# Seven-product blocks in a form with four sums on each side: weight sums chained in one tile by adding DMAs, outputs read from running sums in a bank

## The chip, the cores and the metric

One core of one Trainium2 chip. The metric is device time in microseconds (us), the median of several runs of the whole program; smaller is better. All inputs and outputs are float32.

## The reference, cut to what matters

One decoder layer on 512 tokens with 1024 features: retention and dilated attention side by side, a gated merge, then three steps of which the change touches two:

```python
x = x + (gate_r * ret_branch + gate_a * att_branch) @ w_o      # w_o: 1024 x 1024
u = rmsnorm(x, g_mlp) @ w_up                                   # w_up: 1024 x 4096
x = x + jnp.square(jax.nn.relu(u)) @ w_down                    # w_down: 4096 x 1024
gate_p = jax.nn.sigmoid(rmsnorm(x, g_ple) @ w_ple_gate)
return x + gate_p * (p_i @ w_ple_proj)
```

## The kernel before, in words

**Matrix products.** Each float32 operand is split into a high part rounded to fp32r and a low remainder (`hi`, `lo`). `mm3` (L246) makes a product from three matmuls: high by high (L249), high by low (L250), low by high (L251). A weight tile of 128 x 1024 values, 512 KB, is a unit. `fetch` (L187) loads a unit from HBM on the SP queue into one of six `raw` buffers and can add a second block of the weights to it by an adding DMA on the POOL queue (L202). `split_unit` (L223) then writes the high part on ACT (`whi`, L237) and the low one on DVE (`wlo`, L238), into one of four pairs of buffers. A `raw` buffer comes free when its unit is split, a `whi`/`wlo` pair when the matmuls of its unit are done. `units(n)` (L217) hands out the next n units and splits AHEAD units further (2; 3 at the start of the two blocks with a hand-written order).

**Seven-product blocks.** `w_o` (one block) and `w_down` (four blocks of 1024 rows, f = 0 to 3) are done by blocks of 1024 x 1024 in a scheme in the manner of Strassen: the block is cut into 2 x 2 quadrants, and seven products of sums of quadrants replace eight. One block takes 14 units, here called n0 to n13, two for each product m (u = 0 and u = 1). A unit serves 12 matmuls: two output tiles of 128 tokens (p), two row groups (k) and the three of `mm3`. The left-hand sums are made by `seven_left` (L988) on DVE for each of four column groups j = 0 to 3 (`z`, L991 to L995), then split on ACT (`uh`, L998) and DVE (`ul`, L999). Row groups kk = 0, 1 belong to u = 0, and kk = 2, 3 to u = 1, so the last column group j = 3 is needed by every product's second unit.

In `seven_gemm` (L1001) the order is: products 4, 3 and 5 with u = 0, the same three with u = 1, then 2, 1, 7, 6. Products 2, 7 and 6 go on in the banks of 4, 5 and 3. Product 4 is copied out to SBUF (`m4`, L1040) and product 1 is added to it there (L1054). `acc` (L1026) adds a bank or `m4` to the residual `x` on DVE, with the factor of the token. The weight sums are made by eight adding DMAs per block and by two subtractions of whole raw tiles on DVE (L215, from `differences`).

Before a `w_down` block, four calls of `cols_gemm` (L289) compute w_up's columns; each result goes through Relu and Square on ACT (L1113 to L1122) into `seven_left`.

**Order of the work.** A planner orders the instructions of each engine and queue before the program runs, by its own estimate of when they are ready. In two stretches (the `w_o` block with the embedding product, and the last `w_down` block with the gate product) the ACT and DVE orders are those of the program text; PE, SP and POOL stay with the planner. In these two blocks a finished half row of `x` is handed to `gain_T` (L358), which puts four transposes on PE (`split_T`, L325) and two splits on ACT and DVE (L338, L339) in a list; `tick`, called once every six matmuls in the blocks, takes one due entry from that list.

Of the kernel before, what the change touches and what calls it, by code (L numbers as in the profile page):

```python
# [13 lines left out]
AF = mybir.ActivationFunctionType  # L14
ALU = mybir.AluOpType
AX = mybir.AxisListType

P = 128
# [54 lines left out]
def R(ap):  # L73
    return ap.bitcast(F32R)


class Block:


    def __init__(self, ctx, tc, a):  # L80
# [19 lines left out]
        self.differences = {}  # L100
# [63 lines left out]
    def plan_seven(self, w, r0):  # L164


        q = lambda i, j, u: w[r0 + 512 * i + 256 * u : r0 + 512 * i + 256 * (u + 1), 512 * j : 512 * (j + 1)]
        n = len(self.plan)
        for u in range(2):
            self.plan.append(((q(1, 0, u), q(0, 0, u)), None))  # L170
            self.plan.append(((q(0, 1, u), q(1, 1, u)), None))
            self.plan.append((q(1, 1, u), None))
        for u in range(2):
            self.plan.append((q(0, 0, u), None))
        self.differences[n + 7] = [(n + 6 + u, n + 2 + 3 * u) for u in range(2)]
        for u in range(2):
            self.plan.append(((None, n + 6 + u, n + 2 + 3 * u), None))
        for u in range(2):
            self.plan.append(((q(1, 0, u), q(1, 1, u)), None))
        for u in range(2):  # L180
            self.plan.append(((q(0, 0, u), q(0, 1, u)), None))
# [5 lines left out]
    def fetch(self, n):  # L187
        while len(self.raws) < min(len(self.plan), n):
# [4 lines left out]
            if src is None:  # L193
                self.raws.append((self.raws[add[0]][0], add[1]))
                continue
# [9 lines left out]
    def ahead(self, n):  # L205
        while len(self.loaded) < min(len(self.plan), self.used + n):
            i = len(self.loaded)
            self.fetch(i + 1)
            raw, g0 = self.raws[i]
            src = self.plan[i][0]  # L210
            if isinstance(src, tuple) and src[0] is None:
                g0 = None
            self.loaded.append(self.split_unit(raw, g0))
            for v, w in self.differences.get(i, ()):
                self.nc.vector.tensor_tensor(self.raws[v][0], self.raws[v][0], self.raws[w][0], op=ALU.subtract)  # L215
# [280 lines left out]
    def embed(self):  # L496
# [3 lines left out]
        for half in range(2):  # L500
# [5 lines left out]
            self.rows_gemm(([hi], [lo]), 2, store, bank=self.bank)  # L506
# [421 lines left out]
    def mix(self, A, O):  # L928
        nc = self.nc
        U, Z = [[None] * 4, [None] * 4], {}  # L930
        for pair in ((0, 2), (1, 3)):
            parts = {}
            for br, act, nk, bo in (("a", O, H, 24), ("r", A, KD, 16)):
                if pair[0] and br == "r":
                    self.load_x()
                for cc in pair:
# [9 lines left out]
                    def branch(n, ps):  # L946
# [7 lines left out]
                        if kk < 4:  # L954
# [3 lines left out]
                            nc.scalar.activation(z[:, 1], m[:, :256], AF.Copy)  # L958
                            Z[j] = z, m[:, 256:]
                        else:  # L960
                            z, a21 = Z.pop(j)
                            v = lambda ap: ap.rearrange("p (h t) -> p h t", h=2)
                            nc.vector.tensor_tensor(z[:, 0:8:7], v(t), v(parts[kk]), op=ALU.add)
# [24 lines left out]
    def seven_left(self, z, a21, U, j):  # L988

        nc = self.nc  # L990
        sub = lambda o, x, y: nc.vector.tensor_tensor(o, x, y, op=ALU.subtract)  # L991
# [5 lines left out]
        hi, lo, src = w(U[0][j]), w(U[1][j]), z[:, 1:8].rearrange("p a b -> p (a b)")  # L997
        nc.scalar.activation(R(hi), src, AF.Copy)  # L998
        nc.vector.tensor_tensor(R(lo), src, hi, op=ALU.subtract)  # L999

    def seven_gemm(self, U, xs, f, ready):  # L1001


        nc = self.nc
        LEFT = {1: 3, 2: 4, 3: 0, 4: 6, 5: 1, 6: 5, 7: 2}
        banks = {}

        def product(m, bank, u, first, last):
            (wh, wl), = self.units(1)
            for p in range(2):  # L1010
                if first and m != 1:
                    banks[bank, p] = self.gbank() if m in (3, 4) else self.bank("pb")
                ps = banks[bank, p]
                for k in range(2):
                    kk = 2 * u + k
                    c = slice(LEFT[m] * 256 + p * P, LEFT[m] * 256 + (p + 1) * P)
                    sh, sl = (R(U[i][kk].rearrange("p a b -> p (a b)")[:, c]) for i in range(2))
                    self.mm3(ps, sh, sl, wh[:, k], wl[:, k], first and k == 0, last and k == 1, m != bank)
                self.tick()

        X = lambda i, j, p: xs[2 * i + p][:, 512 * j : 512 * (j + 1)]

        def acc(i, j, p, v, sign=0):
            t, x = 2 * i + p, X(i, j, p)
            c = sign * NT + t
            nc.vector.scalar_tensor_tensor(x, v, f[:, c : c + 1], x, op0=ALU.mult, op1=ALU.add)  # L1026

        def done(i, j, p):
            if ready is not None:
                ready(2 * i + p, j, banks.get((1, p)))  # L1030

        for u in range(2):
            for m in (4, 3, 5):
                product(m, m, u, u == 0, u == 1)
        m4 = []
        for p in range(2):
            banks[1, p] = self.bank("pb")
        for p in range(2):
            t = self.tmp("m4")
            nc.scalar.activation(t, banks[4, p], AF.Copy)  # L1040
            m4.append(t)
            acc(0, 1, p, banks[3, p])
            acc(0, 1, p, banks[5, p], 1)
            done(0, 1, p)
        for u in range(2):
            product(2, 4, u, False, u == 1)
        for p in range(2):
            acc(1, 0, p, banks[4, p])
            done(1, 0, p)
            acc(1, 1, p, banks[4, p], 1)  # L1050
        for u in range(2):
            product(1, 1, u, u == 0, u == 1)
        for p in range(2):
            nc.vector.tensor_tensor(m4[p], m4[p], banks[1, p], op=ALU.add)  # L1054
            acc(0, 0, p, m4[p])
            acc(1, 1, p, m4[p])
        self.AHEAD = 2
        for u in range(2):
            product(7, 5, u, False, u == 1)
        for p in range(2):  # L1060
            acc(0, 0, p, banks[5, p])
            done(0, 0, p)
        for u in range(2):
            product(6, 3, u, False, u == 1)
        for p in range(2):
            acc(1, 1, p, banks[3, p])
            done(1, 1, p)


    def tail(self, mx):  # L1070
# [14 lines left out]
        def ready(t, j, free):  # L1085
            late = (t < 2) == (j == 0)
            if not h2:
                h2.extend(self.new_act(2, "h2"))
            self.gain_T(xs[t], t, j, h2, "h2", 2 * j if late else 1 + t // 2,
                        None if late else (lambda s: free) if t < 2 else self.gbank)  # L1090
# [16 lines left out]
        for f in range(NF // 2):  # L1107
# [3 lines left out]
            def act(b, j, ps):  # L1111
                r = self.tmp("ur")
                nc.scalar.activation(r, ps, AF.Relu)  # L1113
                if b == 0:
# [3 lines left out]
                    nc.scalar.activation(z[:, 1], r[:, :256], AF.Square)  # L1118
                    nc.scalar.activation(a21, r[:, 256:], AF.Square)
                else:  # L1120
                    z, a21 = Z[j]
                    nc.scalar.activation(z[:, 0:8:7], r.rearrange("p (h t) -> p h t", h=2), AF.Square)  # L1122
# [6 lines left out]
            if f == NF // 2 - 1:  # L1129
# [3 lines left out]
                def ready(t, j, free):  # L1133
                    late = (t < 2) == (j == 0)
                    self.gain_T(xs[t], t, j, h3, "h3", 0 if late else 1 + t // 2,
                                None if late else (lambda s: free) if t < 2 else self.gbank)
# [34 lines left out]
    def make_plan(self):  # L1171
# [9 lines left out]
        self.plan_seven(a["w_o"][0], 0)  # L1181
        for half in range(2):
            self.plan_rows(a["w_ple_proj"][0], 512 * half, 2)
        for f in range(NF // 2):
# [3 lines left out]
            self.plan_seven(a["w_down"][0], 1024 * f)  # L1188
# [44 lines left out]
```

## Time and profile before

| what | value |
|---|---|
| time, median of 3 runs | 993.74 us (993.59 to 994.11) |
| profiled execution: span from first to last instruction | 991.8 us |
| PE busy | 984.9 us (99%) |
| DVE busy | 648.8 us (65%) |
| ACT busy | 462.1 us (47%) |
| POOL busy | 98.1 us (10%) |
| mean granted TensorE clock | 0.999 |

The page gives no time of its own for the profiled execution beside its span. The median of the runs is 1.94 us above the span, which is what lies outside the first and last instruction. Matmuls overlap in the pipeline, so a PE that is busy all the time can still lose time between starts: the distance from one start to the next says more than the busy share. `whi<-raw` in a row means that the instruction writes `whi` and reads `raw`; x40 is a count.

### The profile page before, as it was taken

To read this page: it belongs to the slowest core of one execution; us is meant where nothing else is said; L and a number is where in the kernel's file an instruction comes from. 1 tells how busy PE (TensorE), PEld (TensorE's weight loads), DVE (VectorE), ACT (ScalarE), POOL (GpSimd) and SP (SyncE) were. 2 spreads that over 40 slices of the span, in tenths; PEclk is the share of its full clock that TensorE was granted. 3 is DMA by queue.
4 is the path that set the end of the run, shared out by engine and by line. 5 is a ranking of instruction groups with operands and counts; after the bars stand their busy time and mean duration, and the time that the engine had idled before them with its cause. 6 is when DMAs were issued, how large, how long until landed. Compare 5 with 4: busy or idle time off the path is not lost.

```text
span 991.8 us, 12456 instructions
## 1 busy us (share of the span) xinstructions
PE 984.9 (99%) x4588; PEld 826.7 (83%) x4588; DVE 648.8 (65%) x1015; ACT 462.1 (47%) x939; POOL 98.1 (10%) x98
## 2 busy tenths in 40 slices
PE   9999999999999999999999999999999999999998
PEld 6888899889888888888888888888888888888886
DVE  7858675774869345454733796678667769767953
ACT  6635344433334334243423448664563565465451
POOL 0310120220000010001002000100101001000000
PEclk9999999999999999999999999999999999999999
DMA  9723122333234322222446486758749767875911
GB/s 333 262 85 87 44 85 85 113 98 98 83 109 153 124 63 76 96 65 86 162 135 156 137 218 201 185 141 221 184 132 226 187 159 170 228 174 128 298 54 54
DMA packets 90910, 141.16 MB, mean 142 GB/s; under 512 B 6320, under 2 KB 40672, under 8 KB 90848
## 3 DMA queue, kind: packets, MB, share of 16 engines
q1 hardware_dynamic: 79824, 119.36, 37.3%
q0 software_dynamic: 10880, 20.97, 12.6%
q8 instruction: 36, 0.59, 0.2%
q14 instruction: 26, 0.21, 0.1%
q10 hardware_dynamic: 144, 0.02, 0.0%
HBM read 136.10 MB, written 4.24 MB: 141 GB/s over the span
## 4 chain that ended last, share of the span: by engine, by line
PE 97%; DVE 1%; ACT 1%; DMA 1%; SPq 0%; issue 0%; ACTq 0%; DVEq 0%
PE pg L249 27%; PE pg L251 27%; PE pg L250 27%; PE pb L251 3%; PE pb L250 3%; PE pb L249 3%; PE po L699 1%; PE ph L555 1%; PE pt L325 1%; PE sc L676 1%; PE ry L905 1%; PE pe L647 1%; PE kv L893 1%; PE sc L682 1%; PE ry L907 1%; DMA raw<-in_w_in 1%
## 5 line engine op out<-in xcount | busy, mean ns | idle before, releaser
L238 DVE TENSOR_TENSOR wlo<-raw,whi 128x1024 fp32r<-128x1024 f32 (+1 forms) x166 | 196.8, 1190 | 104.3 <-ACT whi L237 102.4
L237 ACT ACTIVATE whi<-raw 128x1024 fp32r<-128x1024 f32 (+1 forms) x165 | 169.7, 1033 | 194.9 <-PE pg L251 71.5
L249 PE MATMUL pg<-whi,hh 128*128 128x512 f32 x440 | 177.3, 403 | 0.0
L251 PE MATMUL pg<-whi,hl 128*128 128x512 f32 x440 | 172.2, 391 | 0.0
L250 PE MATMUL pg<-wlo,hh 128*128 128x512 f32 x440 | 171.9, 391 | 0.0
L251 PEld LDWEIGHTS pg<-whi,hl 128*128 128x128 f32 x440 | 90.4, 206 | 15.1
L249 PEld LDWEIGHTS pg<-whi,hh 128*128 128x128 f32 x440 | 90.5, 206 | 13.8
L250 PEld LDWEIGHTS pg<-wlo,hh 128*128 128x128 f32 x440 | 90.7, 206 | 13.6
L249 PE MATMUL pg<-h2h,whi 128*128 128x512 f32 x256 | 99.6, 389 | 0.0
L250 PE MATMUL pg<-h2l,whi 128*128 128x512 f32 x256 | 99.6, 389 | 0.0
L251 PE MATMUL pg<-h2h,wlo 128*128 128x512 f32 x256 | 99.6, 389 | 0.0
L242 ACT ACTIVATE whi<-raw,gcol 128x256 fp32r<-128x256 f32 (+1 forms) x144 | 66.2, 525 | 22.1 <-PE pg L250 12.4
L243 DVE SCALAR_TENSOR_TENSOR wlo<-raw,gcol,whi 128x256 fp32r<-128x256 f32 (+1 forms) x144 | 65.6, 511 | 15.6 <-ACT whi L242 15.6
L202 POOL DMA_DIRECT2D raw<-in_w_down x32 | 38.6, 1206 | 302.8 <-DMA raw<-in_w_down 188.2
L249 PE MATMUL pg<-hh,whi 128*128 128x512 f32 x160 | 64.0, 400 | 0.0
L249 PE MATMUL pg<-whi,uh 128*128 128x512 f32 x160 | 62.8, 393 | 0.1
L251 PE MATMUL pg<-whi,ul 128*128 128x512 f32 x160 | 62.5, 392 | 0.0
L250 PE MATMUL pg<-wlo,uh 128*128 128x512 f32 x160 | 62.5, 391 | 0.0
L251 PE MATMUL pg<-hh,wlo 128*128 128x512 f32 x160 | 62.4, 390 | 0.0
L250 PE MATMUL pg<-hl,whi 128*128 128x512 f32 x160 | 62.3, 389 | 0.0
L250 PEld LDWEIGHTS pg<-h2l,whi 128*128 128x128 f32 x256 | 48.1, 188 | 10.0
L249 PEld LDWEIGHTS pg<-h2h,whi 128*128 128x128 f32 x256 | 48.1, 188 | 9.9
(201 smaller groups left out, 1693.2 us busy)
## 6 DMA issues: line engine op xcount, KB each, us to landing
raw<-in_w_in SPq DMA_DIRECT2D x72, 512.0 KB, 3.9
raw<-in_w_down SPq DMA_DIRECT2D x48, 512.0 KB, 4.3
raw<-in_w_up SPq DMA_DIRECT2D x32, 512.0 KB, 4.8
raw<-in_w_down POOLq DMA_DIRECT2D x32, 512.0 KB, 6.7
raw<-in_w_o SPq DMA_DIRECT2D x12, 512.0 KB, 3.9
x<-in_x SPq DMA_DIRECT2D x8, 512.0 KB, 6.9
raw<-in_w_ret_out SPq DMA_DIRECT2D x8, 512.0 KB, 3.5
raw<-in_w_o POOLq DMA_DIRECT2D x8, 512.0 KB, 5.8
```

The costliest lines, as they stand in the source:

```text
L202: self.nc.gpsimd.dma_start(raw, rows(add[0]), accum_op=ALU.add)
L237: self.pin(nc.scalar.activation(R(hi[:, i]), raw[:, i], AF.Copy))
L238: nc.vector.tensor_tensor(R(lo[:, i]), raw[:, i], hi[:, i], op=ALU.subtract)
L242: self.pin(nc.scalar.activation(R(hi[:, i]), raw[:, i], AF.Copy, scale=g))
L243: nc.vector.scalar_tensor_tensor(R(lo[:, i]), raw[:, i], g, hi[:, i], op0=ALU.mult, op1=ALU.subtract)
L249: t.matmul(ps, sh, mh, start=first, stop=False, skip_group_check=more)
L250: t.matmul(ps, sh, ml, start=False, stop=False, skip_group_check=more)
L251: t.matmul(ps, sl, mh, start=False, stop=last, skip_group_check=more)
L325: nc.tensor.transpose(ps[:, k * P : (k + 1) * P], part[:, k * P : (k + 1) * P], self.ident)
L555: self.nc.tensor.transpose(ps[:, t * P : (t + 1) * P], rots[t][:, h * HD : (h + 1) * HD], self.ident)
L647: self.nc.tensor.transpose(ps[:, k * P : (k + 1) * P], e[:, k * P : (k + 1) * P], self.ident)
L676: nc.tensor.matmul(sc[:, h * P : (h + 1) * P], qT[:, h, rs], kT[:, h, rs], start=True, stop=True)
```

## The change

- **Order and form of the products.** `seven_products` runs products 1, 5, 2, 6, 3, 7, 4, each with both its units in turn. Products 1, 6, 7, 4 run on in one pair of banks ("b"), 5 and 3 in another ("c"), 2 in a third ("a"). Products 7 and 4 ask for both units at once and finish the first output tile before the second.
- **Outputs.** `after` reads the running sum of a bank straight after a product and adds it to `x` (seven reads for each p; nine operations before), so the next product in that bank waits for the read. The copy `m4` and the addition to it are gone.
- **Left sums.** Four sums in three DVE instructions, two of them `scalar_tensor_tensor`; before, five sums in four instructions.
- **Weight sums.** One tile holds q(0,1) + q(0,0), is split, gets q(1,1) by an adding DMA, is split again, gets q(1,0), and is split a third time (`chained`: the DMA is issued behind the split). The two subtractions on DVE and two plain loads go; eight adding DMAs stay. The two chained tiles keep two of the six raw buffers for the length of the block.
- **Small things.** The column halves are swapped in the plan; AHEAD falls from 3 to 2 after the first product; `gain_T` gets one lag for all; the embedding product takes its banks from the same pool as the block.

```diff
+    def plan_seven(self, w, r0, c1, c2):
+        cols = (c1, c2)
+        q = lambda i, j, u: w[r0 + 512 * i + 256 * u : r0 + 512 * i + 256 * (u + 1), cols[j] : cols[j] + 512]
+        for parts in ([(0, 0)], [(0, 1), (0, 0)], [(1, 0)], (n + 2, (1, 1)), [(1, 1)], [(0, 1), (1, 1)], (n + 2, (1, 0))):
+            for u in range(2):
+                if isinstance(parts, list):
+                    src = tuple(q(*ij, u) for ij in parts)
+                    self.plan.append((src if len(src) > 1 else src[0], None))
+                else:
+                    self.plan.append(((None, parts[0] + u), None))
...
+                    self.chained[last] = (len(self.plan) - 1, q(*parts[1], u))
...
-            for v, w in self.differences.get(i, ()):
-                self.nc.vector.tensor_tensor(self.raws[v][0], self.raws[v][0], self.raws[w][0], op=ALU.subtract)
+            if i in self.chained:
+                self.nc.gpsimd.dma_start(raw, self.chained[i][1].rearrange("(k p) n -> p k n", p=P), accum_op=ALU.add)
...
-            self.rows_gemm(([hi], [lo]), 2, store, bank=self.bank)
+            self.rows_gemm(([hi], [lo]), 2, store)
...
-        sub(z[:, 2], z[:, 1], z[:, 0])
-        sub(z[:, 3:5], z[:, 0:2], z[:, 7:8].to_broadcast([P, 2, 256]))
-        sub(z[:, 5], a21, z[:, 7])
-        sub(z[:, 6], a21, z[:, 1])
+        both = a21.unsqueeze(1).to_broadcast([P, 2, 256])
+        nc.vector.tensor_tensor(z[:, 3:5], z[:, 0:3:2], both, op=ALU.subtract)
+        for o, x, y in ((5, 4, 0), (6, 1, 5)):
+            nc.vector.scalar_tensor_tensor(z[:, o], z[:, x], -1.0, z[:, y], op0=ALU.mult, op1=ALU.subtract)
...
+    SEVEN = ((1, "b"), (5, "c"), (2, "a"), (6, "b"), (3, "c"), (7, "b"), (4, "b"))
+    def seven_products(self, left, after):
+        banks, begun = {}, set()
+        for m, bank in self.SEVEN:
+            whole = m in (7, 4)
+            us = self.units(2) if whole else []
+            for step in range(4):
+                u, p = (step % 2, step // 2) if whole else (step // 2, step % 2)
+                if not whole and p == 0:
+                    us += self.units(1)
+                if (bank, p) not in banks:
+                    banks[bank, p] = self.bank("pa") if bank == "a" else self.gbank()
+                wh, wl = us[u]
+                for k in range(2):
+                    sh, sl = left(m, 2 * u + k, p)
+                    self.mm3(banks[bank, p], sh, sl, wh[:, k], wl[:, k], u == 0 and k == 0 and (bank, p) not in begun,
+                             u == 1 and k == 1, (bank, p) in begun)
+                if u == 1:
+                    begun.add((bank, p))
+                    after(m, p, banks[bank, p])
+                self.tick()
...
+        def after(m, p, v):
+            self.AHEAD = 2
+            for i, j, sign in {1: ((0, 1, 0),), 5: ((1, 0, 1),), 2: ((0, 1, 0),), 6: ((0, 0, 1),), 3: ((0, 0, 1),),
+                               7: ((1, 0, 1),), 4: ((1, 1, 0),)}[m]:
+                t, x = 2 * i + p, xs[2 * i + p][:, 512 * j : 512 * (j + 1)]
+                c = sign * NT + t
+                nc.vector.scalar_tensor_tensor(x, v, f[:, c : c + 1], x, op0=ALU.mult, op1=ALU.add)
+                if ready is not None and m in (2, 3, 7, 4):
+                    ready(t, j)
```

More of the change, by code (lines that the diff above doesn't have):

```diff
@@ L162, in plan_rows @@
             self.plan.append((w[r0 + 256 * u : r0 + 256 * (u + 1), c0 : c0 + 512], None if g0 is None else g0 + 2 * u))
-    def plan_seven(self, w, r0):
-        q = lambda i, j, u: w[r0 + 512 * i + 256 * u : r0 + 512 * i + 256 * (u + 1), 512 * j : 512 * (j + 1)]
+    def plan_seven(self, w, r0, c1, c2):
+        cols = (c1, c2)
+        q = lambda i, j, u: w[r0 + 512 * i + 256 * u : r0 + 512 * i + 256 * (u + 1), cols[j] : cols[j] + 512]
         n = len(self.plan)
[L169 to L181, printed above, removed]
+        for parts in ([(0, 0)], [(0, 1), (0, 0)], [(1, 0)], (n + 2, (1, 1)), [(1, 1)], [(0, 1), (1, 1)], (n + 2, (1, 0))):
[5 more added lines that the diff above has]
+                    self.plan.append(((None, parts[0] + u), None))
+                    last = max(m for m, (p, _) in enumerate(self.plan[:-1])
+                               if m == parts[0] + u or isinstance(p, tuple) and p[0] is None and p[1] == parts[0] + u)
+                    self.chained[last] = (len(self.plan) - 1, q(*parts[1], u))
     def plan_cols(self, w, c0, nk, g0=None):
@@ L193, in fetch @@
             if src is None:
-                self.raws.append((self.raws[add[0]][0], add[1]))
+                self.raws.append((self.raws[add[0]][0], None))
                 continue
@@ L1001, in seven_gemm @@
     def seven_gemm(self, U, xs, f, ready):
         nc = self.nc
[L1005 to L1064, printed above, removed]
@@ L1065, in seven_gemm, with left @@
-        for p in range(2):
-            acc(1, 1, p, banks[3, p])
-            done(1, 1, p)
+        def left(m, kk, p):
+            c = slice(self.LEFT[m] * 256 + p * P, self.LEFT[m] * 256 + (p + 1) * P)
+            return (R(U[i][kk].rearrange("p a b -> p (a b)")[:, c]) for i in range(2))
+        def after(m, p, v):
[7 more added lines that the diff above has]
+                    ready(t, j)
@@ L1070, in tail @@
+        self.seven_products(left, after)
     def tail(self, mx):
@@ L1083, in tail, with ready @@
         left = [2] * NT
-        def ready(t, j, free):
-            late = (t < 2) == (j == 0)
+        def ready(t, j):
             if not h2:
                 h2.extend(self.new_act(2, "h2"))
-            self.gain_T(xs[t], t, j, h2, "h2", 2 * j if late else 1 + t // 2,
-                        None if late else (lambda s: free) if t < 2 else self.gbank)
+            self.gain_T(xs[t], t, j, h2, "h2", 2)
             left[t] -= 1
@@ L1117, in act @@
                     Z[j] = z, a21
-                    nc.scalar.activation(z[:, 1], r[:, :256], AF.Square)
+                    nc.scalar.activation(z[:, 0], r[:, :256], AF.Square)
                     nc.scalar.activation(a21, r[:, 256:], AF.Square)
@@ L1131, in tail, with ready @@
                 halves = [0] * NT
[L1133 to L1136, printed above, removed]
+                def ready(t, j):
+                    self.gain_T(xs[t], t, j, h3, "h3", 1)
                     halves[t] += 1
@@ L1180, in make_plan @@
         self.plan_mix()
-        self.plan_seven(a["w_o"][0], 0)
+        self.plan_seven(a["w_o"][0], 0, 512, 0)
         for half in range(2):
```

17 lines of the change are left out of this document (7 added, 10 removed).

## Prediction

> **What bounds the kernel now.** I read the page first (busy shares, the chain that ended last), then the busy times in five windows, one for each seven-product block, then single instructions in order of time at the two places in these blocks where PE is late.
>
> ```profile
> PE 984.9 (99%) x4588; PEld 826.7 (83%) x4588; DVE 648.8 (65%) x1015; ACT 462.1 (47%) x939; POOL 98.1 (10%) x98
> ```
> ```profile
> PE 97%; DVE 1%; ACT 1%; DMA 1%; SPq 0%; issue 0%; ACTq 0%; DVEq 0%
> ```
> ```profile
> core 0: us, PE busy (x) PEld busy (x) DVE busy (x) ACT busy (x) POOL busy (x), PEclk, DMA share, GB/s
> 558.15:599.90 41.75, 41.66 (x193) 33.65 (x192) 39.21 (x45) 21.15 (x26) 4.83 (x4) 1.00 0.75 197
> 655.23:693.31 38.08, 38.08 (x170) 31.54 (x168) 33.56 (x41) 20.37 (x28) 4.83 (x4) 1.00 0.76 194
> 736.83:775.03 38.20, 38.20 (x170) 31.46 (x168) 32.37 (x38) 20.26 (x28) 4.83 (x4) 1.00 0.75 189
> 818.55:856.63 38.08, 38.08 (x170) 31.54 (x168) 35.59 (x45) 20.48 (x28) 4.82 (x4) 1.00 0.79 205
> 900.15:941.65 41.50, 41.17 (x193) 33.74 (x192) 37.42 (x44) 21.89 (x29) 4.84 (x4) 1.00 0.84 241
> ```
>
> The chain is PE for 97%. The windows say more: a block has 168 weight loads, one for each matmul, and the block from 655.23 takes 38.08 us, 0.2267 us each. The third takes the same and the second 0.12 us more. A unit of twelve matmuls is thus 2.72 us. These three blocks run at PE's own rate, at a granted clock of 1.00, while DVE is busy for 33.56 of 38.08 us. The first and last block hold 24 transposes besides (192 loads); their 3.67 and 3.42 us above 38.08 are transposes and what is lost. The losses that I can point to:
>
> ```profile
> 567.22 0.39 PE L250 MATMUL pg<-wlo,uh 128*128 128x512 f32 x1
> 567.45 0.39 PE L249 MATMUL pg<-whi,uh 128*128 128x512 f32 x1
> 567.67 0.39 PE L250 MATMUL pg<-wlo,uh 128*128 128x512 f32 x1
> 567.90 0.39 PE L251 MATMUL pg<-whi,ul 128*128 128x512 f32 x1
> 568.13 0.39 PE L249 MATMUL pg<-whi,uh 128*128 128x512 f32 x1
> 568.36 0.39 PE L250 MATMUL pg<-wlo,uh 128*128 128x512 f32 x1
> 568.77 0.73 PE L251 MATMUL pg<-whi,ul 128*128 128x512 f32 x2
> ...
> 574.57 0.39 PE L251 MATMUL pb<-whi,ul 128*128 128x512 f32 x1
> 575.02 0.50 PE L249 MATMUL pg<-whi,uh 128*128 128x512 f32 x1
> ```
> ```profile
> 913.55 1.15 DVE raw L215
> ...
> 914.80 1.07 ACT whi L237
> 915.87 0.02 issue
> 915.90 1.23 DVE wlo L238
> 917.12 0.67 DVE x L1026
> ```
>
> Starts 0.23 us apart are the full rate. From 568.36 to the next start are 0.41 us, so 0.18 is lost; at 574.57, 0.45, so 0.22 is lost. The chain in the last block shows a third place: a transposition starts when `x` is ready at 919.06, behind a run of subtraction L215, split and additions to `x`. The matmul before it started at 918.35, so 0.48 us go:
>
> ```profile
> 918.35 0.39 PE L251 MATMUL pg<-whi,ul 128*128 128x512 f32 x1
> 919.06 0.66 PE L325 MATMUL pb<-ident,x 128*128 128x128 f32 x4 [0.33 <-DVE x L1026]
> ```
>
> That makes 0.88 us, and with the 0.12 us of the second block 1.0 us. What is then left of the 3.67 and 3.42 us, 6.2 us for 48 transposes, is 0.13 us each; 1 us of it I keep as a possible loss (an estimate). So about 2 us is the most that any better order in these blocks can win.
>
> **The change, part by part.** *PE.* Seven products of two units of twelve matmuls are 168 before and after; the transposes, eight half rows of four in the first and in the last block, are as many as before. Price 0, and no cover is needed: it is the bound itself.
>
> *DVE, ACT, SP, POOL.*
>
> ```profile
> L215 DVE TENSOR_TENSOR raw<-raw,raw x10: 1215/1219/1225, 572.1 to 914.6; 128x1024 f32<-128x1024 f32 x10
> L1054 DVE TENSOR_TENSOR m<-m,pb x10: 678/682/684, 589.6 to 932.2; 128x512 f32<-128x512 f32 x10
> L1026 DVE SCALAR_TENSOR_TENSOR x<-m,f,x x16: 745/747/753, 685.6 to 933.6; 128x512 f32<-128x512 f32 x16
> L243 DVE SCALAR_TENSOR_TENSOR wlo<-raw,gcol,whi x144: 474/482/752, 601.6 to 968.8; 128x256 fp32r<-128x256 f32 x128, 128x512 fp32r<-128x512 f32 x16
> L202 POOL DMA_DIRECT2D raw<-in_w_down x32: 1203/1203/1222, 621.8 to 921.5; - x32
> ...
> DMA to landing us min/median/max: 5.6/6.0/11.5
> ```
> ```profile
> raw<-in_w_down SPq DMA_DIRECT2D x48, 512.0 KB, 4.3
> ```
>
> Per block DVE loses two subtractions (2 x 1.22), two additions to `m4` (2 x 0.68) and two of sixteen additions to `x` (2 x 0.75): 5.3 us, some 28 of 38 us left. ACT loses the two copies, SP two loads of 512 KB. POOL keeps its eight adding DMAs of 1.20 us. None of this is on the path in the middle blocks, where PE already runs at its rate: worth 0 there. In the first and last block it takes L215 out of the run ahead of the late starts at 575.02 and 919.06. I take both losses as gone, 0.22 + 0.48 = **-0.7 us** (bounds: 0 if the next item on DVE is late instead, -2.0 if all losses go).
>
> *Start of a block.* Before, three products run their u = 0 halves first, so row group 3 is needed only after three units, 8.16 us. Now product 1 asks for it in its second unit, after 2.72 + 0.68 us. Can it be there?
>
> ```profile
> 658.25 1.02 DVE L991 TENSOR_TENSOR z<-z 128x256 f32<-128x256 f32 x2
> 659.18 0.42 DVE L991 TENSOR_TENSOR z<-a,z 128x256 f32<-128x256 f32 x1
> ...
> 659.70 1.71 ACT L998 ACTIVATE uh<-z 128x1792 fp32r<-128x1792 f32 x1 [0.48 <-DVE z L991]
> ...
> 661.43 2.03 DVE L999 TENSOR_TENSOR ul<-z,uh 128x1792 fp32r<-128x1792 f32 x1 [0.70 <-ACT uh L998]
> ```
>
> No: the block began at 655.23, and `ul` of the last column group ends at 663.46, 8.2 us in. The new sums after the last Square are one of 512 columns and two `scalar_tensor_tensor` of 256, serially: about 0.68 + 2 x 0.48 (nearest row L243) = 1.6 us against 1.35 to 1.5 now, no gain. So at its place in the program text row group 3 is some 4.5 us late. What covers it is work of other banks that the planner can put first. The rows from 567.45 show that it does so: after L250 at 567.22 the third matmul of that group (L251, with `ul`) is put off and five matmuls of the other output tile come first. What it can put first without row group 3: product 1's first unit (2.72), half of its second (1.36), the same of product 5 (4.08): 8.16 us, and then product 2's first unit (2.72), once its split is done. That is 10.9 us against 8.2 needed. Where the planner expects `ul` a little too early, the chip waits: it was 0.18 us at 568.77. I take 0.1 us for each of the three middle blocks and for the last, **+0.4 us**.
>
> In the first block, which began at 558.15, the L251 that uses `ul` could start only at 568.77: ready 10.6 us in, against 10.9 of cover; and there the DVE order is that of the text, so the split of n5 stands behind the two additions after product 1, which wait for its end. Product 1's last four matmuls per bank come at about 11 us, the two additions take 1.5, the split of n5 1.2: n5 is ready at 14.4 where PE asks for its low part around 14. **+0.4 us** (bounds 0 and 1.4, the latter if nothing is passed over).
>
> *Chained adding DMAs.* The one for n6 is issued when n2 is split, at about block start (a split is 1.1 us of ACT and 1.2 of DVE, as in the chain above), plus 1.20 us of POOL for the second. With the longest landing, 11.5 us, n6 lies ready at 11.5 and n7 at about 16 us; a split takes 2.3 us; PE wants n6 at 16.3 and n7 at 19.0. Margins 2.5 and 0.7 us at the worst landing, 8 and 6 at the median. The second links are issued when n6 and n7 are split, 14 to 18 us in, and are wanted at 32.6. Price 0; what hides them are the units between. POOL carries the plain adding DMAs for n10 and n11 in the same queue; the buffers for these come free with the splits of n4 and n5 (6 to 14 us in), a load of 4.3 and 6.0 to 11.5 us of adding follow: at most 30 us where n11 is wanted at 28.6, at the median 24. I take 0 and keep 1 us per block for the range. Two of six raw buffers are held, but before n2 and n5 were held as well, until L215.
>
> *Running sums.* Product 4 goes into product 7's bank with no product between; since 7 finishes its first output tile early, DVE has 2.72 us for a 0.75 us read, in a queue that has become shorter. 0 in the middle blocks. In the first and last block the transposes of product 7 come right behind that read, with two splits in the text ahead of it: **+0.1 us** each, +0.2.
>
> Sum: -0.7 + 0.4 + 0.4 + 0.2 = **+0.3 us** on the span of 991.8: 992.1, and with the 1.94 us around it 994.0 us against the median of 993.74. I call that no change: two runs of this kernel can't be told apart below about 0.2%, 2.0 us.
>
> On one point the Trainium skill speaks against the change: TensorE: Matmul & The Clock Gate, section Part 2, states that matmuls stay in program order in PE's queue and that only weight loads are pulled ahead. By that, any wrong guess of the planner's is paid in full, and with product 1 left where the text has it the sum would be that of the first rival. The trace agrees as to the queue: at 568.36 the matmuls behind the late L251 waited too.
>
> **The rivals.** *PE stands at each block's start (slower).* The planner keeps product 1 together. Then PE waits for `ul` from 3.85 us into the block (2.72 and five matmuls of 0.2267) to 8.3: 4.4 us in four blocks, and 10.6 - 3.85 = 6.7 in the first, 24 us in all: 1018 us. It decides from the point where less than 4.4 us of other matmuls is put ahead. Against it: the rows from 567.45. For it: the three u = 0 halves at the head were the whole cover so far.
>
> *The planner passes, but misses more often.* It has 16 groups of transposes and five starts to place; with the largest miss seen, 0.48 us, at eleven of them instead of three, the blocks lose 11 x 0.48 = 5.3 against 0.88 now: 998 us; at seven, 996.2.
>
> *An adding DMA is late.* n11 by 1 to 1.5 us in each of five blocks: 5 to 7.5 us, near 1000 us; in one or two blocks about 996. Against it: the median of 6.0.
>
> *All losses go (faster).* -2.0 us at most, 991.8 us, just at the edge of what can be told; for it speaks DVE's shorter queue.
>
> **How the numbers follow.** No change as summed (992.3 to 995.7): 0.56. All losses go: 0.20, of which 0.04 goes past 0.2%. More misses: 0.10, slower. Late DMA: 0.07, of which 0.04 slower. PE standing: 0.07. So faster 0.04, same 0.75, slower 0.21. The range leaves out the standing PE and the far ends of the misses and late DMAs: 992.0 to 997.0, with the likeliest case alone at 992.3 to 995.7.
>
> **What would show each step.** Right: windows of 38.1 to 38.3 us for the middle blocks; at a block's head a change of bank after some 18 matmuls instead of 24; additions to `x` on PSUM only; landing of the adding DMAs unchanged. Wrong: a gap between matmul starts at 3 to 8 us into a block, released by `ul`; waits of `whi` on adding DMAs above today's; a transposition released by `x` with more than 0.5 us of idle PE.

## The result and the profile after: 1.3% slower

The changed kernel takes 1006.43 us (median; 1005.04 to 1009.57), the kernel before on the same chip 993.73 us (993.59 to 994.11). The ratio is 1.0133, with a 95% interval of 1.0117 to 1.0150. The forecast was 994.0 us. In the profiled execution the span grew from 991.8 to 1005.2 us, by 13.4 us.

Line numbers of the changed kernel differ from those of before: the splits are L231 (ACT) and L232 (DVE), the transposes L319, the additions to `x` L1033, plain adding DMAs L199, chained ones L209, the left sums L986 and L988, `uh` and `ul` L991 and L992, the three matmuls of `mm3` L243 to L245.

From the page of the kernel after, the busy shares and the chain that ended last:

```profile
PE 989.5 (98%) x4588; PEld 828.4 (82%) x4588; DVE 620.1 (62%) x965; ACT 455.9 (45%) x929; POOL 98.4 (10%) x98
...
PE 89%; DMA 4%; DVE 2%; issue 2%; ACT 2%; POOL 0%; SPq 0%; ACTq 0%; POOLq 0%; DVEq 0%
```

PE executes the same 4588 matmuls, and DVE lost 28.7 us of work and ACT 6.2 us. Yet the chain, which was PE for 97%, is PE for 89% now, and DMA has 4% of it. The same windows as in the prediction, one for each seven-product block:

```profile
557.61:605.61 48.00, 43.62 (x194) 35.42 (x192) 35.14 (x40) 21.07 (x29) 7.20 (x6) 0.93 0.70 167
660.95:699.42 38.47, 38.40 (x169) 31.39 (x168) 30.84 (x39) 18.84 (x25) 7.24 (x6) 1.00 0.90 206
742.94:781.41 38.47, 38.40 (x170) 31.39 (x168) 30.85 (x39) 18.83 (x25) 7.25 (x6) 1.00 0.90 207
824.93:863.42 38.49, 38.43 (x170) 31.41 (x169) 30.75 (x39) 18.83 (x25) 7.23 (x6) 1.00 0.90 206
906.94:955.05 48.11, 43.59 (x194) 34.62 (x192) 32.49 (x41) 22.24 (x32) 8.33 (x8) 0.96 0.76 197
```

The number behind each window is the block's length, the one before the DMA share the granted clock. The first block lost 6.25 us and the last 6.61; the middle ones lost 0.39, 0.27 and 0.41. Together that is 13.9 us, and the first block began 0.55 us earlier: 13.4, all of the difference.

**The first block.** POOL's instructions, then the chain of work in order of time:

```profile
569.20 1.20 POOL L199 DMA_DIRECT2D raw<-in_w_o  x1 [6.34 <-DMA raw<-in_w_o]
574.32 2.44 POOL L209 DMA_DIRECT2D raw<-in_w_o  x2 [3.91 <-DVE wlo L232]
576.93 1.22 POOL L199 DMA_DIRECT2D raw<-in_w_o  x1 [0.17 <-issue]
```
```profile
576.93 10.54 DMA raw<-in_w_o
...
587.58 1.06 ACT whi L231
...
589.81 0.76 DVE x L1033
...
590.61 1.12 PE pt L319 x4
591.72 0.43 PE pg L243
```

Over the whole run the plain adding DMAs (first line) and the chained ones (second) land hardly later than the 5.6/6.0/11.5 us of before:

```profile
DMA to landing us min/median/max: 5.6/6.4/10.5
```
```profile
DMA to landing us min/median/max: 5.5/5.8/12.1
```

Unit n11's raw buffer got its load 14 us into the block, and its adding DMA was third on POOL, behind two chained ones. It landed 10.54 us after its issue, 29.9 us into the block. By itself that would have cost about 2.2 us (an estimate: PE had done 120 matmuls of the block when it stopped, and six more could run without n11, until 587.45; its high part was ready at 588.64, 1.2 us later, and its low part at 589.88, 1.0 us behind the start that its second matmul was then due). But in the text order of ACT and DVE the split of n11 stands ahead of the addition to `x` behind product 3, and a transposition on PE waits for that addition. The view of the waits in this block names both ends of it:

```profile
ACT whi L231 <- DMA raw<-in_w_o: 6.9, 1, 6.9
...
PE pt L319 <- DVE x L1033: 4.4, 1, 4.4
```

And after the wait the matmuls came 0.43 us apart instead of 0.227. Windows of PE alone (length, busy time and count, granted clock, DMA share, GB/s) show why:

```profile
585.80:590.60 4.80, 0.44 (x2) 0.78 0.67 247
590.60:595.27 4.67, 4.66 (x15) 0.50 0.38 112
...
936.35:938.59 2.24, 0.01 (x1) 1.00 0.43 167
...
936.60:940.02 3.42, 1.43 (x9) 1.00 0.45 154
940.02:943.43 3.41, 3.41 (x12) 0.50 1.05 396
...
946.30:948.54 2.24, 0.02 (x2) 1.00 0.45 115
...
946.84:950.26 3.42, 1.72 (x10) 1.00 0.72 204
```

PE stood 4.5 us, and while it stood the granted clock fell to one half; it came back at 595.27. The stretch at half clock lost another 2.3 us of its 4.67. In the last block PE stood 2.24 us, 1.43 us later the clock was halved for 3.41 us (1.7 us lost), and then PE stood 2.24 us again. (Counted from the start that was due 0.23 us behind the last one, the three waits are 4.5, 2.4 and 2.4 us; the losses below are counted so.) The Trainium skill, in TensorE: Matmul & The Clock Gate, section Part 1, tells of half clock after an idle window of about 3.4 us, with windows that run freely. The length of 3.41 us agrees; that a whole window must be idle does not, since 2.24 us sufficed at 936.35, while 2.24 us at 946.30 did not. The traces show what decides. Within each of them the stretches at half clock begin whole multiples of 3.413 us apart, and on that grid the window 936.60:940.02 had 1.99 us of idle PE, while the second wait lay across a boundary and left 1.70 us in 946.84:950.26. In the sixteen traces of this case every window of the grid with 1.88 us or more of idle PE was followed by half clock, and none with 1.87 us or less (e13, 942.56:945.97).

**The last block.** The chain holds the same story at its start, and a second one at its end:

```profile
926.40 9.05 DMA raw<-in_w_down
935.56 1.07 ACT whi L231
...
937.79 0.76 DVE x L1033
938.59 0.66 PE pt L319 x4
...
944.12 1.06 ACT whi L231
...
946.35 1.22 DVE wlo L232
...
947.83 0.67 DVE x L1033
948.54 0.66 PE pt L319 x4
```

The second wait is no DMA's: the addition behind product 7 stands behind the splits of n12 and n13, and these stand on ACT behind the split of a half row that had just been transposed (943.63). `gain_T` gives a lag of 1 there: a half row's transposes come due one `tick` after it is ready.

**The middle blocks.** DVE at the head of the last block, which looks as in the middle ones:

```profile
910.67 0.42 DVE L988 SCALAR_TENSOR_TENSOR z<-z 128x256 f32<-128x256 f32 x1
911.01 1.22 DVE L232 TENSOR_TENSOR wlo<-raw,whi 128x1024 fp32r<-128x1024 f32 x1
912.15 0.42 DVE L988 SCALAR_TENSOR_TENSOR z<-z 128x256 f32<-128x256 f32 x1
914.39 2.03 DVE L992 TENSOR_TENSOR ul<-z,uh 128x1792 fp32r<-128x1792 f32 x1 [1.83 <-ACT uh L991]
```

The second of two sums needs the first one's result, and the planner put a split of 1.22 us into the time between them. So `uh` and `ul` come about 1 us later, and PE loses 0.34 us some 7 us into each of the last four blocks.

### The profile page after: what moved, and what is told of

Its sections match the earlier page's. It is cut to its first block, busy times and chain, and to the rows that moved or that the text cites. A ratio compares the mean times of both kernels' runs of the same rounds, so it can differ in the third digit from the quotient of the medians.

```text
span 1005.2 us, 12390 instructions
## 1 busy us (share of the span) xinstructions
PE 989.5 (98%) x4588; PEld 828.4 (82%) x4588; DVE 620.1 (62%) x965; ACT 455.9 (45%) x929; POOL 98.4 (10%) x98
## 4 chain that ended last, share of the span: by engine, by line
PE 89%; DMA 4%; DVE 2%; issue 2%; ACT 2%; POOL 0%; SPq 0%; ACTq 0%; POOLq 0%; DVEq 0%
PE pg L243 26%; PE pg L244 26%; PE pg L245 26%; DMA raw<-in_w_o 2%; DMA raw<-in_w_down 1%; ACT uh L991 1%; DVE wlo L232 1%; PE po L693 1%; PE ph L549 1%; PE pt L319 1%; PE sc L670 1%; PE ry L899 1%; PE pe L641 1%; ACT whi L231 1%; PE pa L245 1%
## 5 line engine op out<-in xcount | busy, mean ns | idle before, releaser
L232 DVE TENSOR_TENSOR wlo<-raw,whi 128x1024 fp32r<-128x1024 f32 (+1 forms) x166 | 196.2, 1190 | 111.2 <-ACT whi L231 110.0
L231 ACT ACTIVATE whi<-raw 128x1024 fp32r<-128x1024 f32 (+1 forms) x165 | 168.9, 1031 | 185.6 <-PE pg L245 78.5
L243 PE MATMUL pg<-whi,hh 128*128 128x512 f32 x440 | 177.3, 403 | 0.0
L245 PE MATMUL pg<-whi,hl 128*128 128x512 f32 x440 | 172.2, 391 | 0.0
L245 PEld LDWEIGHTS pg<-whi,hl 128*128 128x128 f32 x440 | 90.4, 205 | 15.0
L244 PEld LDWEIGHTS pg<-wlo,hh 128*128 128x128 f32 x440 | 90.7, 206 | 13.7
L243 PEld LDWEIGHTS pg<-whi,hh 128*128 128x128 f32 x440 | 90.5, 206 | 13.8
L243 PE MATMUL pg<-h2h,whi 128*128 128x512 f32 x256 | 99.6, 389 | 0.0
L245 PE MATMUL pg<-h2h,wlo 128*128 128x512 f32 x256 | 99.6, 389 | 0.0
L243 PE MATMUL pg<-whi,uh 128*128 128x512 f32 x240 | 95.9, 400 | 0.3
L244 PE MATMUL pg<-wlo,uh 128*128 128x512 f32 x240 | 94.8, 395 | 0.0
L245 PE MATMUL pg<-whi,ul 128*128 128x512 f32 x240 | 92.5, 395 | 0.0
L243 PE MATMUL pg<-hh,whi 128*128 128x512 f32 x160 | 64.0, 400 | 0.0
L245 PE MATMUL pg<-hh,wlo 128*128 128x512 f32 x160 | 62.4, 390 | 0.0
L243 PEld LDWEIGHTS pg<-h2h,whi 128*128 128x128 f32 x256 | 48.0, 188 | 10.0
L245 PEld LDWEIGHTS pg<-h2h,wlo 128*128 128x128 f32 x256 | 48.0, 188 | 9.9
```

The source lines that it names most:

```text
L231: self.pin(nc.scalar.activation(R(hi[:, i]), raw[:, i], AF.Copy))
L232: nc.vector.tensor_tensor(R(lo[:, i]), raw[:, i], hi[:, i], op=ALU.subtract)
L243: t.matmul(ps, sh, mh, start=first, stop=False, skip_group_check=more)
L244: t.matmul(ps, sh, ml, start=False, stop=False, skip_group_check=more)
L245: t.matmul(ps, sl, mh, start=False, stop=last, skip_group_check=more)
```

## The experiments

The theories: L, the late adding DMA of n11 reaches the transposes through the text order; T, the text order alone does it; T2, the lag holds the second wait in the last block, against S, the splits hold it whatever the lag; H, the planner's guess of `uh` at a block's head; H2 and H3, the split between the two sums, or their serial latency; C and D, the adding DMAs are stretched by the next stage's loads, or by one another. All lengths of blocks are from the start of the first matmul to 0.23 us behind the start of the last, in the profiled execution; times are medians (the profiled execution of e13, 1002.25 us, is the fastest of its four).

| kernel | blocks, us | time, us | ratio to before (95%) |
|---|---|---|---|
| before | 41.75, 38.08, 38.20, 38.08, 41.50 | 993.73 | |
| after | 48.00, 38.47, 38.47, 38.49, 48.11 | 1006.43 | 1.0133 (1.0117 to 1.0150) |
| e1 | 41.46, 38.55, 38.47, 38.49, 43.43 | 996.66 | 1.0033 (1.0020 to 1.0046) |
| e2 | 41.31, 38.49, 38.50, 38.47, 44.05 | 997.31 | 1.0036 (1.0023 to 1.0049) |
| e3 | 43.99, 38.50, 38.47, 38.49, 42.64 | 998.75 | 1.0053 (1.0038 to 1.0068) |
| e4 | 44.35, 38.49, 38.48, 38.48, 45.65 | 1001.43 | 1.0087 (1.0058 to 1.0117) |
| e5 | 41.29, 38.46, 38.49, 38.53, 41.66 | 994.58 | 1.0006 (0.9997 to 1.0015) |
| e6 | 41.26, 39.07, 38.49, 38.49, 42.19 | 995.29 | 1.0016 (1.0007 to 1.0025) |
| e7 | 41.28, 38.46, 38.47, 38.46, 43.65 | 997.84 | 1.0037 (1.0023 to 1.0051) |
| e8 | 41.27, 38.51, 38.47, 38.46, 41.65 | 994.02 | 1.0001 (0.9992 to 1.0010) |
| e9 | 42.73, 39.95, 38.08, 38.08, 41.25 | 995.77 | 1.0023 (1.0014 to 1.0032) |
| e10 | 41.27, 40.85, 42.52, 42.59, 41.58 | 1004.11 | 1.0100 (1.0084 to 1.0115) |
| e11 | 41.27, 38.08, 38.08, 38.08, 44.65 | 996.59 | 1.0029 (1.0018 to 1.0041) |
| e12 | 41.25, 39.57, 40.08, 40.23, 42.35 | 999.89 | 1.0065 (1.0052 to 1.0077) |
| e13 | 45.93, 38.50, 38.46, 38.50, 45.18 | 1005.03 | 1.0113 (1.0097 to 1.0129) |
| e14 | 41.29, 38.08, 38.08, 38.08, 41.29 | 992.03 | 0.9984 (0.9975 to 0.9993) |

**e1: one unit more ahead in the two blocks with a written order.**

```diff
-            self.AHEAD = 3
+            self.AHEAD = 4        # and the same at the gate product
```

> AHEAD is 4 instead of 3 at the head of the two hand-ordered blocks, so that n5's split stands ahead of product 1's additions in the ACT and DVE text. Theory L (the adding DMA of n11 is late, since its raw buffer comes free only when n5 is split, and its lateness reaches the transposes through the text order): n11's load goes out 2 to 3 us earlier, its adding DMA gets ahead of the chained ones, both blocks fall from 48 us to about 42.5; 994 to 997 us. Theory T (the text order itself, splits and lags ahead of the additions, holds the transposes whenever the DMAs come): no change, 1004 to 1008.

The first block is back at 41.46, the last comes down by 4.7 us, and the half clock is gone. What remains in the last is the second wait, here 1.7 us, in e1's chain:

```profile
933.79 1.06 ACT whi L231
...
936.02 1.22 DVE wlo L232
...
937.49 0.67 DVE x L1033
...
938.21 0.66 PE pt L319 x4
```

Most of the loss hangs on when n11 is ready, as L says.

**e2: n10 and n11 loaded without their second block.**

```diff
-        for parts in (..., [(1, 1)], [(0, 1), (1, 1)], (n + 2, (1, 0))):
+        for parts in (..., [(1, 1)], [(0, 1)], (n + 2, (1, 0))):
```

> n10 and n11 are loaded plain: the second block of the weights, q(1,1), is not added to them, so product 7 is of other numbers; ten adding DMAs go, everything else stays. L: both long waits of the transposes go, the clock stays at 1.00; blocks of 41.5 to 42.5 us, 993 to 996 us. T: the second wait in the last block (2.4 us) and most of the first stay; 1001 us or more.

The first block is cured without any change of order (41.31), so the text order alone (T) does no harm there; it only passes on what is late. The last block keeps its second wait, 2.16 us at 938.6. Of the 30 adding DMAs left none took over 9 us to land (longest 8.86); with all 40 it was 7 of them, up to 12.09. The kernel before has 7 such landings too, up to 11.50: late landings are not new, but which unit has one is, and what stands behind it. Product 7 is of other numbers in e2, so it is a test and no version of the layer.

**e3: no written order in the two blocks.**

```diff
-        with self.tc.manual_schedule(engines={nc.scalar.engine, nc.vector.engine}):
+        with ExitStack():
```

> ACT and DVE are left to the planner in the two blocks too. L: n11 still lands as late, but only its own matmuls wait for it, no addition to x stands behind its split: 1 to 2 us per block, 995 to 999 us. T: 993 to 996, all waits of transposes gone. If the wait were due to the late DMA alone and the text order passed nothing on: no change, 1005.

Both blocks improve, but transpositions still wait, 1.22 and 0.97 us in the first block and 0.33 us in the last. But the planner also put n11's adding DMA ahead of the second chain links (575.35 in the first block, landed at 582.20; 918.25 and 923.93 in the last), so n11 was in time here. That its lateness would cost less without the text order is not shown by e3.

**e4: n11's adding DMA ahead of the second chain links on POOL.**

```diff
-                    self.chained[last] = (len(self.plan) - 1, q(*parts[1], u))
+                    late = parts[1] == (1, 0)
+                    self.chained.setdefault(n + 11 if late else last, []).append((last, q(*parts[1], u), late))
...
```

> The second links of the chain (n12, n13) are issued on POOL behind the adding DMA of n11, in all five blocks, instead of straight after the splits of n6 and n7. L: n11's adding DMA goes out as soon as its load has landed and without two others in flight (6 instead of 10.5 us): lands 4 to 5 us earlier in both blocks, waits of the transposes fall to under 1 us; 994 to 998 us. T: no change. If the buffer that comes free late is all of it and the queue nothing: lands under 1 us earlier, 1003 or more.

n11 landed in 5.54 us and its wait went. But the second link of n13 is now the last of three, and it takes n11's place in the chain:

```profile
579.90 12.61 DMA raw<-in_w_o
...
592.59 1.07 ACT whi L234
...
596.23 0.66 PE pt L322 x4
```

Which adding DMA is late depends on the order; the third in this row is late in both.

**e5: e1 with a lag of 2 in the last block. e6: e1 with the splits of n12 and n13 behind product 7's first addition.**

```diff
-                    self.gain_T(xs[t], t, j, h3, "h3", 1)
+                    self.gain_T(xs[t], t, j, h3, "h3", 2)     # e5
```
```diff
+            if m == 7:
+                self.AHEAD = 0                                # e6
...
+                    if m == 7 and p == 0:
+                        self.ahead(self.AHEAD)
```

> e1 (AHEAD 4) and in the last block lag 2 instead of 1 for the transposes, as in the first block. Of the 3.1 us that e1's span still has over before, 1.9 us are one wait of a transposition in the last block. Theory T2 (with lag 1 the evacuation of the transposition before stands in the ACT text ahead of the splits of n12 and n13, and these stand ahead of product 7's addition): the wait falls under 0.4 us, the last block from 43.4 to 41.5 to 42 us; 994.5 to 995.5 us. Rival S (the splits ahead of the addition hold it whatever the lag): 43 us or more, 996.5.

> e1 and in both blocks the splits of n12 and n13 behind product 7's first addition in the text; lag 1 stays. T2 and S both: the wait of the transposition before product 7's second half goes; last block 41.5 to 42.3 us, 994.5 to 995.5 us. If the splits of n12 and n13 then come too late for product 4: a wait of PE for whi or wlo of 1 us or more in its place.

The lag brings the last block to 41.66 us, within 0.16 of before. Moving the splits gives 42.19, 0.5 us more; that edit reaches all blocks, and in the first middle one (39.07) a matmul at 687.78 waits for an addition to `x`. T2 holds, and S falls.

**e7: the u = 0 halves of products 1, 5 and 2 first, as before the change. e8: the same with lag 2.**

```diff
...
+        first, rest = self.SEVEN[:3], self.SEVEN[3:]
+        for (m, bank), steps in [(mb, (2 * u, 2 * u + 1)) for u in range(2) for mb in first] + [(mb, range(4)) for mb in rest]:
...
```

> The changed kernel with the u = 0 halves of products 1, 5 and 2 ahead of their u = 1 halves in text and plan, all five blocks; AHEAD 3 and lag 1 stay. Theory H (the 0.34 us at 7 us into each block come from the planner's guess of when uh is ready): middle blocks 38.1 instead of 38.5 us. Theory L: n5's split now stands ahead of product 1's addition, n11's load goes out as early as in e1: first block about 41.5 us. The wait of 1.9 us in the last block stays (T2). 995 to 996 us. Rival: the late buffer comes back another way and the blocks stay above 44 us.

> e7 with lag 2 in the last block. H, L and T2 together: all five blocks within 0.3 us of before (41.4, 38.1, 38.1, 38.1, 41.4); 993.0 to 994.0 us, no slower than before. If one of the three is wrong its block keeps its loss: 1.3 us for H, 6 for L, 1.9 for T2.

The order of the products is not what holds the middle blocks: with the old cover they still take 38.46 to 38.51 us, and 0.36 us is now waited for `ul`. H falls. But in this order n11's adding DMA goes ahead of the second links on POOL and lands at 580.82, 6.7 us earlier than in the kernel after, and the first block is cured without AHEAD 4. e8 is as fast as before.

**e9 and e10: in e8 and in e5, n4's split behind the second sum.**

```diff
+                if behind is not None:
+                    self.tc.add_manual_dep(low.ins, behind.ins.name, ..., reason="behind the left sums")
```

> e8, and in every block the low part of n4 is kept behind the last left sum in DVE's order. Theory H2 (what is left, 0.36 us at 9 us into each w_down block, comes from the planner putting that split of 1.22 us between the two serial sums of the last column group, so that ul ends 1 us later than before): middle blocks 38.1 instead of 38.5 us, 992.3 to 993.3 us. Rival H3 (the two sums are serial now, and that latency alone makes ul late): 38.3 us or more, no change against e8.

> The same edit on e5 (products in the order of the change). H2: uh ends 1 us earlier and the wait of 0.34 us at 7 us into the blocks goes; middle blocks 38.1 us, 992.6 to 993.8 us. H3: 38.4 us as in e5, 994.5 us.

Where nothing else intervened the middle blocks of e9 took 38.08 us, PE's own rate: the split between the sums (H2) was their loss. The price was paid elsewhere. In e9 a transposition of the first block waited 1.41 us (576.63), and n11's adding DMA of the first middle block took 8.93 us; in e10 the one of the next block was third on POOL again, with n10's, issued at 750.62, still in flight:

```profile
753.59 1.13 POOL raw L211
...
754.73 1.24 POOL raw L211
...
756.67 11.52 DMA raw<-in_w_down
...
768.29 1.06 ACT whi L233
...
770.66 0.50 PE pg L249
```

So the late unit stops PE also without the text order and without transposes: n11 landed 29.05 us into this block, its first two matmuls came 1.40 and 1.03 us late, and a half clock of 3.41 us followed at 771.40. Why the planner's order moved there by a dependency at the block's head wasn't followed up.

**e11, e12 and e13: the next stage's first three loads on POOL, behind the adding DMAs** (e11 on e9, e12 on e10, with n4's split held back in the four `w_down` blocks alone; e13 on the kernel after, in the first block alone).

```diff
-            self.nc.sync.dma_start(raw, rows(src))
+            if len(self.raws) in self.patient:                # units n+14, n+15, n+16
+                self.tc.keep_in_program_order(self.nc.gpsimd.dma_start(raw, rows(src)))
+            else:
+                self.nc.sync.dma_start(raw, rows(src))
```

> e9 with the low part of n4 kept behind the sums in the four w_down blocks alone, and the loads of the three units after each block issued on POOL behind the block's adding DMAs instead of on SP beside them. Theory C (the adding DMAs land late, up to 12 us instead of 6, because three of them and the next stage's loads are in flight together): no adding DMA of n10 to n13 lands after more than 9 us, no wait for one, all middle blocks 38.1 us, first and last 41.3; 991.8 to 993.0 us, faster than before by 0.1 to 0.2%. Rival D (the adding DMAs stretch each other, and the plain loads have no part in it): landings of 9 us and more stay, a block or two keeps 1 to 4 us, 994 to 998 us. If the loads now come too late for the next stage: PE waits after the block's end, not in it.

> The same two edits on e10 (products in the order of the change, AHEAD 4, lag 2). C: the waits of 1 to 2.7 us for n11 in e10's middle blocks and the slower clock behind them go; 38.1 us each, 992 to 993.5 us. D: 997 us or more.

> The kernel after the change, with one thing moved: behind the first block (w_o) the next three loads (two of w_ple_proj, one of w_up) are issued on POOL in text order behind n11's adding DMA instead of on SP. In the kernel after, n11's adding DMA was the third on POOL (two chained links at 574.32 and 575.46, its own at 576.93) and landed 10.54 us after its issue, with these three loads in flight from 579.57, 581.30 and 583.75. Theory C (the loads share the transfer and stretch the adds): without the loads the three adds come out some 2.55 us apart, as in the runs before where nothing else was in flight (760.84, 763.37, 765.94), so n11 lands about 585.0 instead of 587.5; PE then stands 1.9 us instead of 4.4 at the transposition, its clock stays or is halved for 3.4 us instead of 6.8; first block 42 to 45 us instead of 48.0, the last block unchanged at about 48.1; time 1000.5 to 1003.5. Theory D (the adds stretch one another, the loads have no part): n11 lands again 10 to 10.7 us after its issue, first block 47.5 to 48.5, time 1006 or more if the loads now come late.

e11 is cured in four blocks: in the first middle block n11's adding DMA, first in its row, lands in 5.70 us instead of 8.93, and the second chain link behind it in 8.09 instead of 11.63. In its last block two loads of 1 MB on SP were in flight, and n11's took 10.11. e12 is not cured: there n11's is the third of a row, and it still took 10.61 us in the third block. In e13 it came 9.10 us after its issue, between what C (8.1) and D (10 to 10.7) said:

```profile
577.70 9.10 DMA raw<-in_w_o
...
589.94 0.66 PE pt L325 x4
```

But e13 decides less than it was meant to. The loads on POOL went out behind its issue, not behind its landing: 3.0, 4.8 and 7.2 us after it, against 2.6, 4.4 and 6.8 in the kernel after, so they were in flight beside it all the same. And the spacing of 2.55 us on which C's figure rests is that of e12, where such loads were in flight too (from 756.06). The last block, whose code e13 leaves as it was, took 45.18 us instead of 48.11, with n11's landing in 6.87 us instead of 9.05: landings of the same code differ by 2 us between executions, so 1.4 us at n11 speaks for neither theory. In e11, too, the loads were in flight with the adding DMAs (issued at 674.71 to 677.34, behind n11's at 673.25; in e9 at 673.08 to 678.01, one of them ahead of n11's at 675.07). Whether POOL's queue or the order of the issues helped there is not shown.

All 470 adding DMAs of before, after and e1 to e10, sorted by what was in flight, go with both theories (median us from issue to landing, and how many; "beside" is the mean number of transfers other than adding DMAs in flight during the landing):

| earlier adding DMAs not yet landed | under 1 beside | 1 to 2 beside | 2 or more beside |
|---|---|---|---|
| 0 | 5.8 (186) | 6.9 (14) | 8.4 (3) |
| 1 | 6.0 (139) | 7.8 (33) | 9.4 (6) |
| 2 | 7.9 (12) | 9.4 (31) | 11.0 (13) |
| 3 | 9.5 (2) | 11.1 (7) | 12.1 (24) |

With two earlier ones it is 2 us more, and with loads beside them 1.5 to 3 more. This sorts what happened; no run took the loads away and left the row of adding DMAs as it was.

**e14: e11 with the loads of the last block back on SP.**

> The version of the three runs on u = 0 halves first, lag 2 in the last block and the second left sum ahead of n4's split, with the next stage's three loads on POOL behind the adds, but now in the first four blocks alone: in the last block they go back to SP. In the run with all five blocks so, four blocks took 41.27, 38.08, 38.08 and 38.08 us and the last 44.65, because its second pair of adding DMAs stood in one POOL queue beside two loads of 1 MB; with the loads of the last block on SP it took 41.25. If late weight sums (L), the lag (T2), the split between the serial sums (H2) and the loads in flight (C) are all there is, the blocks take 41.3, 38.1, 38.1, 38.1 and 41.3, together 196.8 against 197.6 before, and with the same time around them the kernel takes 992 to 993.5 us, ratio 0.998 to 0.9995. If the loads moved to POOL cost the next stage as much as they win here (D and others), a stage behind a block becomes longer by over 1 us and the time is 994 to 996.

```profile
PE 99%; DVE 0%; ACT 0%; issue 0%
```
```profile
558.27:599.55 41.28, 41.28 (x193) 33.60 (x192) 35.23 (x40) 21.19 (x29) 8.37 (x8) 1.00 0.76 194
654.89:692.97 38.08, 38.08 (x169) 31.53 (x168) 30.65 (x39) 18.73 (x25) 8.39 (x8) 1.00 0.84 208
```

With the four edits together every block runs at PE's rate, and the kernel takes 992.03 us, 0.16% less than before (interval 0.07 to 0.25%). This is the one version that beats both. Whether the kernel before would win as much by an order of its own wasn't tried.

## Why the prediction was wrong, point by point

- **The step that failed: "Chained adding DMAs", price 0, range 1 us per block.** The bound was worked out rightly: "at most 30 us in where n11 is wanted at 28.6". It came so: 29.9 us in the first block, 28.5 in the last. Wrong was to take the median landing instead of asking what is in flight at that moment; and to hold the landing itself against 28.6, without the 2.3 us of the split that were counted for n6 and n7, so that even the last block's 28.5 is late. The change puts two chained links on POOL right ahead of n11's adding DMA, and the next stage's loads beside them. The page of before had the numbers for it:

```profile
q1 hardware_dynamic: 79824, 119.36, 37.3%
q0 software_dynamic: 10880, 20.97, 12.6%
```

  The 40 adding DMAs hold 12.6% of the 16 engines for 991.8 us, so 3.1 us each (an estimate); 512 KB of the plain loads, by the same rows, hold 1.6 us. Three adding DMAs and three loads within 10 us are 14 us of transfer by that estimate; in the first block they were issued from 574.32 to 583.75 and had landed at 590.25. The prediction read the landing as a property of one DMA, and it is a queue.

- **The same step, its second half: how lateness is passed on.** What would have cost about 2.2 us by itself became 4.5 us of idle PE in the first block, since the split of n11 is ahead of an addition in the text, and a transposition is ahead of other matmuls in PE's queue. (In e10, without the text order, a landing 29.05 us in cost 2.4 us.) The prediction followed what stands behind the split of n5, not behind that of n11. And idle PE halved the granted clock, 2.3 and 1.7 us more, which no step had. The term was 0; it measured 6.8 us in the first block and about 4.1 in the last. The rival "An adding DMA is late" had the mechanism with 1 to 1.5 us in each of five blocks, and a chance of 0.07.

- **Transposes of product 7, "+0.1 us each".** Right in kind (two splits in the text ahead), wrong in size: 2.4 us in the last block. Those splits stood behind a split of a transposition on ACT, a chain that the prediction did not follow. With lag 2 it is gone (e5).

- **Start of a block, "+0.1 us each".** It measured 0.34 us in each of the last four blocks, and its cause was another: not a wrong guess of the planner's but a split of 1.22 us between two serial sums (e7 against e9). The prediction counted the sums as 1.6 us and left out that other work can go between them. The rival of a PE that stands for 4.4 us did not come: the planner passed over product 1 in every block.

- **First block, "+0.4 us" for n5's split behind product 1's additions.** The terms 11, 1.5 and 1.2 make 13.7 and not 14.4; the order was as said (569.02 additions, 570.34 split of n5), and the split ended 13.95 us in. PE's cost there was under 0.3 us; the worse effect, that n5's split frees n11's raw buffer, stood in the working ("6 to 14 us in") and got no price.

- **Right:** the count of matmuls and transposes; the time that DVE (28.7 us, said 5.3 in each of five blocks) and ACT lose, and that it is worth nothing where PE is the bound; running sums at no price in the middle blocks; and that about 2 us is the most a better order can win: e14 wins 1.7.

## What to carry to other kernels

Price a DMA by the queue that it meets: what is issued just ahead of it and beside it, times the engines' time of each, not by a median landing. Where a margin is negative in the worst case, follow what stands behind the late instruction, engine by engine, until PE, and add what PE's clock does after it stood. A change that frees an engine off the path gains nothing, and its new places in the queues can cost.

## What the runs showed of the hardware

- An adding DMA of 512 KB took 5.5 to 5.8 us from issue to landing when alone, up to 13.5 us as the fourth in a row with loads beside it (e3), and by the rows of the queues about twice the engine time of a plain load (an estimate). The Trainium skill, in DMA: Bandwidth & Descriptors, section Issuing engines are not separate DMA queues, says that DMAs of all engines end on the same 16 DMA engines and interleave; the table above agrees, and so does e13, where three loads moved from SP to POOL were in flight beside n11's adding DMA as before.
- An idle PE of 2.24 us was followed once by 3.41 us of half clock and once by none; 4.5 us idle by a half clock that began within the wait and ended 4.7 us after it. What decided in all sixteen traces was the idle time within one window of a fixed 3.413 us grid: 1.88 us or more was followed by half clock, 1.87 or less was not.
